# One half of the stream kept on chip between two layers, with two smaller moves, in a two-layer encoder kernel

## The chip, the core and the metric

The kernel runs on one core of a Trainium2 chip. The core has five engines that work side by side, each in its own order: TensorE (PE, matrix products; its weight loads are listed as PEld), VectorE (DVE), ScalarE (ACT), GpSimd (POOL) and SyncE (SP, which here only issues DMA transfers). Transfers are also issued by POOL, and only POOL issues those that add into DRAM while they write. The metric is the device time of one execution in microseconds (us), median over runs. TensorE's clock is granted by a throttle, and the profile shows it as a share of full speed.

## The reference

A float32 stream x of 1024 tokens by 1024 features goes through two layers. Each layer has a mixer and an MLP, both behind an RMSNorm and both added to the stream. Layer 0's mixer is a gated linear recurrence, layer 1's a forgetting attention; in both a 4-head attention into 256 memory tokens stands beside it, and both groups read one projection of the normed stream.

```python
for layer in range(DEPTH):
    h = rms_norm(x, norm_mix[layer])
    y_mix, xq = rglru_group(h, ...) if layer == 0 else fox_group(h, ...)
    y_mem = memory_group(xq, mem, ...)       # keys, values: rms_norm(mem) @ w_kv
    x = x + jnp.concatenate([y_mix, y_mem], axis=-1) @ w_out[layer]
    h = rms_norm(x, norm_mlp[layer])
    x = x + jnp.square(jax.nn.relu(h @ w_mlp_in[layer])) @ w_mlp_out[layer]
```

## The kernel before, in words

**Layout.** The stream is held transposed: 8 row tiles of 128 features, each with two halves of 512 tokens (`H = 512`). Between the stages it lies in DRAM, in `xs` (the tile is named `xspill` in the profile), and is loaded by `load_x`, one row tile and one half at a time (128x512 float32, 256 KB). On chip such tiles live in 86 slots (`NU`), which the float32 tiles `f` and the split tiles `r` share; `get` takes a slot that has been free long, `put` gives it back, and the next user of a slot waits for its last reader.

**Products.** Float32 accuracy is made from three products of split operands: each operand is a high part (`split`, L488: an ACT copy that rounds and applies the norm's gain) and a low part (the rest, made on DVE or POOL, L491 and L499). For weights the same is done in a ring of three buffers, `wh` by ACT (L319) and `wl` by DVE or POOL (L320), from four raw buffers `wr`, which SP fills from DRAM (L315, about one load per weight row). TensorE's result goes to PSUM banks in four groups: `pspj` (2 banks), `pss` (2), `pspt` (3), `pso` (1).

**Norms.** RMSNorm's gain is applied when x is split, its factor 1/rms per token after the product. Sums of squares come in three ways. `sqacc` squares a tile on ACT (L441) and adds it to a running sum on DVE or POOL (L447). `sq_pe` squares on ACT (L452) and lets TensorE add, by products of 128x128 with a column of 1/D (`sq_mm`, L465, 4 narrow products a tile, into a `pso` bank); it keeps the newest two squares back and multiplies those before. `tok_sums` (L469) loads the stream with tokens on the partitions (`xtok`, an input) and lets ACT sum the squares along the row. `norm_fin` turns the sums into the factor and spreads it over the partitions by a scaled identity, made on POOL (L530), and a product with ones (L381).

**Order of the stages.** Layer 0: first half normed and projected (`in_u0`, `in_g0`), recurrence, memory attention, second half, output projection, MLP. Beside `in_g0` the generator `norm_split(1, ...)` (L541) loads and splits the second half of x, and at its end `tok_sums` sums that half's squares; `norm_fin(1, True)` (L1659) follows after the first half's recurrence. The MLP runs in 8 groups of 512 hidden features. Each group multiplies by two 2x2 block matrices in 7 products in place of 8 (operands b11, b21, t2, t3, t1, t4, b22, which are sums and differences of blocks made on DVE): `mlp_z` for the first matrix, `mlp_out` for the second. In `mlp_out` each quarter of the result gets two products: `first` copies the one from PSUM to an `f` slot (L1075, on ACT), `then` adds the other (`plus`, L1080, on DVE), and `send` (L1219) adds the sum into `xs` in DRAM by an accumulating transfer that POOL issues (L1220). So the stream after the last group of layer 0 stands in DRAM alone.

**The seam between the layers.** The generator `kv(1)` makes the memory's keys and values for layer 1 (K: 8 weight rows of 512 columns and products with the normed memory, then norm and transposes; V likewise). It starts inside the last MLP group and is taken 6 steps further at L1682; the rest is woven with `norm_split_back` (L553), which loads the first half of x from `xs` row by row (L538), splits it behind the newest weight split (L488), and sums its squares. Then comes the first projection of layer 1, the memory query (`xq_proj`).

**Who sets the order.** The program is written in stages and generators (`weave`, `advance`, `drain`), but a scheduler then orders each engine's instructions by a modelled time; `after` adds a fixed order between two instructions. So an edit in one place can move instructions far from it.

## Time and profile before

| | us |
|---|---|
| median of 3 runs (lowest, highest) | 2108.54 (2106.35, 2111.91) |
| the profiled execution, and its span | 2108.65, 2106.9 |
| PE busy | 2055.2 (98% of the span), 10378 products |
| DVE busy | 1564.0 (74%) |
| ACT busy | 1154.3 (55%) |
| POOL busy | 463.3 (22%) |
| mean granted clock of TensorE | 0.988 |

Engine totals count busy time over the whole span. Times in the traces run from the span's start. A row of the timeline has start, length, engine, line, operation, tiles, count and, in brackets, how long the engine waited before it and for whom. A row of the waits has who waited for whom, the sum, the count and the longest. A window row is explained where the first one stands.

### The profile page before, as it was taken

The numbers are of one execution on the slowest core, as the hardware profiler recorded it, in microseconds if no ns is written. First come the engines' busy times: TensorE is split into PE (matmuls) and PEld (weight loads), VectorE is DVE, ScalarE is ACT, GpSimd is POOL, SyncE is SP. The second block draws the span as 40 slices with busy tenths as digits, with TensorE's granted clock in tenths as the row PEclk, the third lists the DMA queues.
The fourth block names the chain that finished last, engine by engine and source line by source line (L and its number), as shares of the span: only waits on it lengthen the run. The fifth ranks groups of instructions, "written<-read, shape, count | busy, mean of one in ns | idle before, by whom it ended". The sixth has DMA issues, their size and how long they took to land. (4 is left out here: it accounts for less than half of the span.)

```text
span 2106.9 us, 29666 instructions
## 1 busy us (share of the span) xinstructions
PE 2055.2 (98%) x10378; PEld 1712.8 (81%) x10378; DVE 1564.0 (74%) x2916; ACT 1154.3 (55%) x2172; POOL 463.3 (22%) x590
## 2 busy tenths in 40 slices
PE   9999999999999999997999999999999999999999
PEld 7987788888788888876998998777778888888887
DVE  8878698776776776785585778787787768658757
ACT  7756656554554554555464655576554555445544
POOL 1132210201201201214252333232012122022021
PEclk9999999999999999998899999999999999999999
DMA  7433362635635635748568437743446674365374
GB/s 276 151 99 117 101 195 76 130 81 110 131 81 110 135 77 109 160 94 246 192 232 295 151 100 267 239 149 117 145 101 140 139 179 95 80 147 99 78 184 120
DMA packets 122646, 301.56 MB, mean 143 GB/s; under 512 B 13760, under 2 KB 15872, under 8 KB 122496
## 3 DMA queue, kind: packets, MB, share of 16 engines
q1 hardware_dynamic: 79584, 209.41, 29.6%
q0 software_dynamic: 42912, 90.26, 22.8%
q8 instruction: 81, 1.33, 0.3%
q14 instruction: 69, 0.57, 0.1%
HBM read 190.46 MB, written 109.15 MB: 142 GB/s over the span
## 5 line engine op out<-in xcount | busy, mean ns | idle before, releaser
L1064 PE MATMUL pspt<-r,wh 128*128 128x512 f32 x1536 | 491.6, 396 | 1.0 <-ACT wh L319 1.0
L320 DVE TENSOR_TENSOR wl<-wr,wh 128x1024 fp32r<-128x1024 f32 (+2 forms) x354 | 337.9, 965 | 198.0 <-ACT wh L319 196.9
L319 ACT ACTIVATE wh<-wr 128x1024 fp32r<-128x1024 f32 (+3 forms) x403 | 304.5, 777 | 296.4 <-PE pss L1064 73.2
L1220 POOL DMA_DIRECT2D xspill<-f x240 | 212.1, 1111 | 854.8 <-DVE f L1080 825.1
L1064 PEld LDWEIGHTS pspt<-r,wh 128*128 128x128 f32 x1536 | 288.3, 188 | 71.5 <-ACT wh L319 1.4
L1064 PE MATMUL pss<-r,wh 128*128 128x512 f32 x1024 | 329.1, 396 | 0.4 <-DVE r L499 0.4
L1064 PE MATMUL pspt<-r,wl 128*128 128x512 f32 x768 | 304.0, 396 | 0.0
L1064 PE MATMUL pspj<-r,wh 128*128 128x512 f32 x832 | 272.1, 399 | 1.0 <-DVE r L491 1.0
L388 PE MATMUL pspj<-wh,r 128*128 128x256 f32 (+1 forms) x1280 | 252.5, 290 | 15.3 <-ACT r L488 11.7
L499 DVE TENSOR_TENSOR r<-f,r 128x512 fp32r<-128x512 f32 x282 | 191.0, 696 | 75.9 <-DMA xspill<-f 61.3
L1064 PEld LDWEIGHTS pss<-r,wh 128*128 128x128 f32 x1024 | 192.1, 188 | 48.5 <-DVE r L499 0.8
L388 PEld LDWEIGHTS pspj<-wh,r 128*128 128x128 f32 x1280 | 207.1, 194 | 19.7 <-ACT r L488 13.0
L496 ACT ACTIVATE r<-f 128x512 fp32r<-128x512 f32 x282 | 169.6, 625 | 82.8 <-DMA xspill<-f 25.1
L1064 PE MATMUL pss<-r,wl 128*128 128x512 f32 x512 | 202.4, 395 | 0.0
L1064 PEld LDWEIGHTS pspj<-r,wh 128*128 128x128 f32 x832 | 156.6, 189 | 39.8 <-DVE r L491 1.8
L388 PE MATMUL pspj<-wl,r 128*128 128x256 f32 (+1 forms) x640 | 184.9, 289 | 0.2 <-POOL wl L320 0.2
L1064 PEld LDWEIGHTS pspt<-r,wl 128*128 128x128 f32 x768 | 144.5, 188 | 35.2
L1064 PE MATMUL pspj<-r,wl 128*128 128x512 f32 x416 | 164.9, 397 | 0.0
L388 PE MATMUL pspj<-r,wh 128*128 128x512 f32 x480 | 157.8, 404 | 3.9 <-DVE wr L836 1.7
L1085 ACT ACTIVATE f<-f 128x512 f32<-128x512 f32 x128 | 78.8, 626 | 105.1 <-DVE f L1084 102.8
L388 PEld LDWEIGHTS pspj<-wl,r 128*128 128x128 f32 x640 | 123.7, 193 | 1.2 <-POOL wl L320 0.4
L1064 PEld LDWEIGHTS pss<-r,wl 128*128 128x128 f32 x512 | 96.2, 188 | 23.8 <-issue 0.5
(301 smaller groups left out, 3570.2 us busy)
## 6 DMA issues: line engine op xcount, KB each, us to landing
wr<-in_w_dram SPq DMA_DIRECT2D x136, 512.0 KB, 3.9
xspill<-f POOLq DMA_DIRECT2D x240, 256.0 KB, 7.2
f<-xspill SPq DMA_DIRECT2D x88, 256.0 KB, 4.6
xspill<-f SPq DMA_DIRECT2D x48, 256.0 KB, 3.1
wsp<-wh SPq DMA_DIRECT2D x22, 512.0 KB, 5.7
wsp<-wl SPq DMA_DIRECT2D x22, 512.0 KB, 6.1
wh<-wsp POOLq DMA_DIRECT2D x21, 512.0 KB, 5.2
wl<-wsp POOLq DMA_DIRECT2D x21, 512.0 KB, 5.4
```

The lines of the kernel that those rows point to most:

```text
L319: self.wact = self.nc.scalar.activation(hi, raw, AF.Copy)
L320: eng.tensor_tensor(lo, raw, hi.bitcast(F32), ALU.subtract)
L388: self.lastmm = self.nc.tensor.matmul(out, lhsT=a, rhs=b, start=(j == 0), stop=(j == n - 1))
L496: i = self.nc.scalar.activation(hi[:, :n], src, AF.Copy)
L499: self.nc.vector.tensor_tensor(lo[:, :n], src, hi[:, :n].bitcast(F32), ALU.subtract)
L1064: self.lastmm = self.nc.tensor.matmul(ps, lhsT=a, rhs=b, start=(start and c == 0 and j == 0), stop=(c == n - 1 and j == 2), skip_group_che ...
L1085: self.lastsq = self.nc.scalar.activation(f[:, n], f[:, n], AF.Square)
L1220: nc.gpsimd.dma_start(self.xs[2 * q + a, :, b * H:(b + 1) * H], f[:, n], accum_op=ALU.add)
```

## The change

It has three parts.

1. *First half's result stays on chip.* In the last MLP group of layer 0, when the first matrix is at its operand t1 (`hook7`), the eight row tiles of the first half are loaded from `xs` into `xres`. The two quarters of the result with b = 0, which are these tiles, are then not copied and sent: `held` adds both products into the resident tile on DVE, and the sum is written to `xs` by a plain transfer that SP issues. `norm_split_back` takes the resident tiles and loads nothing. `kv` is taken 2 steps ahead instead of 6.
2. *Second half's row sums.* `tok_sums` issues all its loads first, each into a slot of its own, and then squares. For the second half it is called at the start of `in_g0`, behind the newest weight split on ACT, in place of the end of `norm_split`. `norm_fin(1, True)` moves from behind the first half's recurrence into `in_g0`.
3. *Sums of squares.* `sq_pe` no longer multiplies; it only squares and queues. The narrow products are placed by hand: in layer 0 at operands b11 and b21 of the MLP's first matrix, in layer 1 before and behind the waiting product (`drain(p)` in `mlp`: one MLP group's first matrix, begun ahead of the MLP, that still waits for the last operands of the second half), and the rest in `norm_fin_g`. The `pso` bank is taken when the first of them is made.

```diff
--- before.py
+++ after.py
@@ -218,6 +218,7 @@
         self.parked = {}
         self.stp = {}
         self.tst = {}
+        self.xres = {}
         self.xg = [None, None]
         self.ymix = [None, None]
         self.hs = [None, None]
@@ -453,11 +454,12 @@
         if behind is not None:
             self.after(i, behind)
         if m == 0:
-            self.stp[h] = self.psum("o"), []
+            self.stp[h] = [None, []]
         self.stp[h][1].append((m, sq))
-        self.sq_mm(h, 2)
 
     def sq_mm(self, h, keep):
+        if self.stp[h][0] is None:
+            self.stp[h][0] = self.psum("o")
         st, todo = self.stp[h]
         while len(todo) > keep:
             m, sq = todo.pop(0)
@@ -469,15 +471,17 @@
     def tok_sums(self, src, n, tag, behind=None):
         nc = self.nc
         st = self.small(2 * n, tag, 1)
+        xs = [self.F.get() for _ in range(2 * n)]
+        for k, x in enumerate(xs):
+            nc.sync.dma_start(x[:, :H], src[k // 2, :, k % 2 * H:(k % 2 + 1) * H])
         for t in range(n):
             for j in range(2):
-                x = self.F.get()
-                nc.sync.dma_start(x[:, :H], src[t, :, j * H:(j + 1) * H])
+                x = xs[2 * t + j]
                 i = nc.scalar.activation(x[:, :H], x[:, :H], AF.Square, scale=1.0 / math.sqrt(D),
                                          accum_out=st[:, j * n + t:j * n + t + 1])
                 if behind is not None:
                     self.after(i, behind)
-                self.F.put(x)
+        self.F.put(*xs)
         return st
 
     def tok_var(self, v, st, n):
@@ -538,7 +542,7 @@
         self.nc.sync.dma_start(x[:, :H], src[k, :, h * H:(h + 1) * H])
         return x
 
-    def norm_split(self, h, g, src, stats, tok=None):
+    def norm_split(self, h, g, src, stats):
         xs = self.xg[h] = []
         for k in range(8):
             x = self.load_x(k, h, src)
@@ -547,14 +551,12 @@
             xs.append(self.split(x[:, :H], self.pc(g, k)))
             self.F.put(x)
             yield
-        if tok is not None:
-            self.tst[h] = self.tok_sums(tok[4 * h:4 * h + 4], 4, f"tst{h}", self.last_hi)
-
-    def norm_split_back(self, h, g, src):
+
+    def norm_split_back(self, h, g):
         nc = self.nc
         xs = self.xg[h] = [None] * 8
         for j, k in enumerate((0, 2, 4, 6, 1, 3, 5, 7)):
-            x = self.load_x(k, h, src)
+            x = self.xres.pop(k)
             xs[k] = self.split(x[:, :H], self.pc(g, k), behind=self.wact)
             self.sqacc(j, h, x[:, :H], nc.vector, self.last_hi)
             self.F.put(x)
@@ -1226,7 +1228,20 @@
             nc.sync.dma_start(self.out[2 * q + a, :, b * H:(b + 1) * H], f[:, n])
             self.F.put(f)
 
+        def held(a):
+            def first(q, ps):
+                self.plus(self.xres[2 * q + a], ps)
+
+            def then(q, ps):
+                x = self.xres[2 * q + a]
+                self.plus(x, ps)
+                nc.sync.dma_start(self.xs[2 * q + a, :, :H], x[:, n])
+
+            return first, then
+
         def keep(a, b):
+            if b == 0 and self.xres:
+                return held(a)
             dst = []
 
             def first(q, ps):
@@ -1274,19 +1289,25 @@
         def hook0(key):
             if key in ahead:
                 self.xsplit(ahead[key])
+            if key in ("b11", "b21"):
+                self.sq_mm(1, 6 if key == "b11" else 3)
             if key in ("t2", "t3"):
                 advance(nf)
 
         def hook7(key):
             if key == "t2" and nxt is not None:
                 advance(nxt)
+            if key == "t1" and not l:
+                self.xres = {m: self.load_x(m, 0, self.xs) for m in (0, 2, 4, 6, 1, 3, 5, 7)}
             if key == "t1" and l:
                 self.acc = [self.load_x(2 * q, 0, self.xs) for q in range(4)]
 
         for p in wait:
             for k in ("t3", "t1"):
                 self.xsplit(k)
+            self.sq_mm(1, 5)
             drain(p)
+            self.sq_mm(1, 2)
         for g in range(8):
             if g == 0 and g in self.parked:
                 for k in ("t3", "t1"):
@@ -1591,7 +1612,7 @@
 
 
         xk = self.ins["xtok"]
-        nrm = [self.norm_split_first(0, "gmix0", xT, xk), self.norm_split(1, "gmix0", xT, False, xk)]
+        nrm = [self.norm_split_first(0, "gmix0", xT, xk), self.norm_split(1, "gmix0", xT, False)]
         advance(nrm[0])
         kv = self.kv(0)
 
@@ -1623,7 +1644,10 @@
                     yield
 
         def in_g0():
+            self.tst[1] = self.tok_sums(xk[4:], 4, "tst1", self.wact)
             for m in range(4):
+                if m == 2:
+                    self.norm_fin(1, True)
                 for _ in range(4):
                     advance(kv)
                     yield
@@ -1656,7 +1680,6 @@
         weave(self.xq_proj(0), lru0, TUNE["xq0"])
         drain(lru0)
         self.xg_free(0)
-        self.norm_fin(1, True)
         xa0 = self.xattn(0)
         weave(self.xq_proj(1), xa0, TUNE["xq1"])
         weave(in_u1(), xa0, TUNE["in_u1"])
@@ -1679,8 +1702,8 @@
 
 
         self.fox_setup()
-        advance(kv, 6)
-        weave(kv, self.norm_split_back(0, "gmix1", self.xs), 1.0)
+        advance(kv, 2)
+        weave(kv, self.norm_split_back(0, "gmix1"), 1.0)
         self.vst = {}
         xq = self.xq_proj(0, 1)
         advance(xq, 4)
```

The lines behind the edits move by one to four: L1080 is L1082 in the changed kernel, L499 is L503, L488 is L492, L530 is L534.

**Where it moves instructions: DVE in the last group of layer 0's MLP.** The rows are DVE's order, from the place where the second matrix's first products are out. Names are tile, generation, number; L1188 to L1196 before (L1187 to L1198 in the changed kernel) make the operand sums, L499 (L503) their low parts, L320 (L321) and L629 (L631) low parts of weights and of the memory, L1082 is the plus. Before:

```order
L1188 TENSOR_TENSOR f40_835_7958<-f21_824_7841,f7_816_7732 128x512
L1194 TENSOR_TENSOR f41_834_7954<-f21_824_7841,f41_834_7954 128x512
L320 TENSOR_TENSOR wl2_78<-wr0_69,wh2_75 128x1024
L1188 TENSOR_TENSOR f8_839_7980<-f53_825_7855,f83_817_7746 128x512
L1194 TENSOR_TENSOR f37_838_7976<-f53_825_7855,f37_838_7976 128x512
L629 SCALAR_TENSOR_TENSOR r9_853_8086<-f81_818_7782,par_79,r51_852_8085 128x256 x2
L1196 TENSOR_TENSOR f60_822_7808<-f60_822_7808,f40_835_7958 128x512
L499 TENSOR_TENSOR r17_855_8092<-f7_816_7732,r56_854_8091 128x512
L499 TENSOR_TENSOR r11_857_8096<-f83_817_7746,r52_856_8095 128x512
L499 TENSOR_TENSOR r75_837_7961<-f40_835_7958,r76_836_7960 128x512
```

In the changed kernel four pluses into resident tiles stand among the operand sums:

```order
L1082 TENSOR_TENSOR f41_830_7865<-f41_830_7865,pss_397_8006 128x512
L1187 TENSOR_TENSOR f12_816_7732<-f8_842_7970,f12_816_7732 128x512
L1082 TENSOR_TENSOR f22_832_7869<-f22_832_7869,pspj_399_8008 128x512
L503 TENSOR_TENSOR r53_841_7953<-f15_823_7822,r30_840_7952 128x512
L1082 TENSOR_TENSOR f39_831_7867<-f39_831_7867,pss_398_8007 128x512
L1187 TENSOR_TENSOR f31_817_7746<-f5_846_7992,f31_817_7746 128x512
L1082 TENSOR_TENSOR f48_833_7871<-f48_833_7871,pspj_400_8009 128x512
L1190 TENSOR_TENSOR f71_843_7974<-f20_824_7841,f12_816_7732 128x512
```

and directly behind them:

```order
L1196 TENSOR_TENSOR f8_842_7970<-f20_824_7841,f8_842_7970 128x512
L321 TENSOR_TENSOR wl2_78<-wr0_69,wh2_75 128x1024
L631 SCALAR_TENSOR_TENSOR r11_857_8098<-f67_818_7782,par_79,r52_856_8097 128x256 x2
L503 TENSOR_TENSOR r72_859_8104<-f12_816_7732,r73_858_8103 128x512
L1190 TENSOR_TENSOR f54_847_7996<-f84_825_7855,f31_817_7746 128x512
L1196 TENSOR_TENSOR f5_846_7992<-f84_825_7855,f5_846_7992 128x512
L503 TENSOR_TENSOR r62_861_8108<-f31_817_7746,r61_860_8107 128x512
L1082 TENSOR_TENSOR f41_830_7865<-f41_830_7865,pspt_401_8051 128x512
L1198 TENSOR_TENSOR f37_822_7808<-f37_822_7808,f71_843_7974 128x512
L1082 TENSOR_TENSOR f39_831_7867<-f39_831_7867,pspt_402_8052 128x512
L1082 TENSOR_TENSOR f22_832_7869<-f22_832_7869,pspt_403_8053 128x512
L503 TENSOR_TENSOR r19_845_7977<-f71_843_7974,r78_844_7976 128x512
```

The split that ends the last list (`r19`) is the one that ends the first (`r75` there). It now stands 19 rows behind the first plus, and seven of these rows are pluses; before, no plus stood ahead of it.

**ACT at the seam.** The rows are ACT's order around the split of the first rows of x for layer 1 (L488, its square L441). Before, they follow the key transposes' copies (L677), one row of x after another:

```order
L677 ACTIVATE r72_929_8748<-pspt_425_8745,gkq_409_8343 128x256
L677 ACTIVATE r39_930_8754<-pspt_426_8751,gkq_409_8343 128x256
L488 ACTIVATE r32_912_8598<-f63_911_8596,par_79 128x512
L441 ACTIVATE f36_914_8602<-f63_911_8596 128x512
L488 ACTIVATE r63_916_8620<-f36_915_8618,par_79 128x512
L441 ACTIVATE f0_918_8624<-f36_915_8618 128x512
L488 ACTIVATE r36_920_8643<-f0_919_8641,par_79 128x512
L441 ACTIVATE f37_922_8647<-f0_919_8641 128x512
```

In the changed kernel the splits (L492, L442) read the resident tiles `f41`, `f39`, `f22` and stand among the memory's copies and the weight splits (L320) of the key/value stage:

```order
L492 ACTIVATE r0_888_8395<-f41_830_7865,par_79 128x512
L442 ACTIVATE f33_890_8399<-f41_830_7865 128x512
L1077 ACTIVATE f44_883_8332<-pspj_400_8009 128x512
L492 ACTIVATE r41_891_8414<-f39_831_7867,par_79 128x512
L442 ACTIVATE f65_893_8418<-f39_831_7867 128x512
L601 ACTIVATE f26_885_8354<-pspt_411_8366 128x256
L320 ACTIVATE wh0_73<-wr3_72 128x256 x2
L603 ACTIVATE f27_887_8392<-f26_885_8354 128x256
L320 ACTIVATE wh0_73<-wr3_72 128x256
L492 ACTIVATE r65_895_8437<-f22_832_7869,par_79 128x512
L442 ACTIVATE f49_897_8441<-f22_832_7869 128x512
L320 ACTIVATE wh0_73<-wr3_72 128x256
```

All eight pairs moved in front of the key transposes.

**POOL in layer 0's first projection.** The rows are POOL's order around the scaled identity of the second half's norm (L530, L534 in the changed kernel); L890 and L901 belong to the recurrence, L706 to the memory attention's query. Before:

```order
L890 TENSOR_SCALAR f77_136_1207<-f77_136_1207 128x512
L706 TENSOR_TENSOR f68_129_1174<-f68_129_1174,xr_109_1516 128x512
L706 TENSOR_TENSOR f69_130_1175<-f69_130_1175,xr_109_1516 128x512
L706 TENSOR_TENSOR f33_131_1176<-f33_131_1176,xr_109_1516 128x512
L706 TENSOR_TENSOR f72_132_1177<-f72_132_1177,xr_109_1516 128x512
L890 TENSOR_SCALAR f63_133_1201<-f63_133_1201 128x512
L530 TENSOR_SCALAR f38_157_1546<-ident_81,rst1_112_1534 128x128 x4
L901 TENSOR_SCALAR f63_133_1201<-f63_133_1201 128x512
```

In the changed kernel:

```order
L534 TENSOR_SCALAR f35_105_888<-ident_81,rst1_83_876 128x128 x4
L892 TENSOR_SCALAR f34_135_1225<-f34_135_1225 128x512
L892 TENSOR_SCALAR f85_136_1227<-f85_136_1227 128x512
L892 TENSOR_SCALAR f0_137_1229<-f0_137_1229 128x512
L892 TENSOR_SCALAR f71_134_1223<-f71_134_1223 128x512
L903 TENSOR_SCALAR f71_134_1223<-f71_134_1223 128x512
```

The four scaled identities now stand ahead of the recurrence's rows.

## The prediction

> **What bounds the kernel now.** I read the page's engine totals first, then the stages in 40 us windows, then PE's waits, and last the two engines around the places that stood out.
>
> ```profile
> PE 2055.2 (98%) x10378; PEld 1712.8 (81%) x10378; DVE 1564.0 (74%) x2916; ACT 1154.3 (55%) x2172; POOL 463.3 (22%) x590
> PEclk9999999999999999998899999999999999999999
> ```
>
> TensorE is busy for 2055.2 of 2106.9 us, so only 51.7 us are plain waiting, and the clock row dips in just one place, a little before the middle. The windows (columns: stretch, its length, busy time and count for PE, PEld, DVE, ACT, POOL, then granted clock, DMA share, GB/s) put both in one stage:
>
> ```profile
> 960.00:1000.00 40.00, 27.07 (x193) 24.44 (x193) 24.97 (x52) 22.58 (x60) 14.78 (x16) 0.83 0.80 259
> 1000.00:1040.00 40.00, 36.25 (x256) 35.63 (x255) 19.60 (x53) 14.61 (x40) 9.82 (x10) 0.79 0.47 169
> ```
>
> This is the seam between the layers: memory keys and values of layer 1, then the first query projection. PE idles 12.9 us in the first window, and the clock is low in both. The list of PE's waits names the cause, and the waits of 920 to 1060 us say what stands behind it (us, times, longest):
>
> ```profile
> PE pspj L388 <- ACT r L488: 11.7, 4, 5.4
> PE pso L381 <- POOL f L530: 3.1, 1, 3.1
> PE pso L465 <- ACT f L452: 2.8, 1, 2.8
> ACT r L488 <- DMA f<-xspill: 23.1, 7, 7.1
> SPq L538 <- DVE f L447: 21.9, 5, 7.9
> ```
>
> PE waits for the split of x (L488), the split for its load from DRAM, and the load for a buffer: only one slot is free, and it comes back when DVE has added the previous square (L447). So one row of x after another makes a round trip, while the clock falls to half:
>
> ```profile
> 990.00:995.00 5.00, 2.93 (x12) 2.63 (x12) 1.35 (x2) 1.24 (x2) 0.00 (x0) 0.50 0.99 345
> 1010.00:1015.00 5.00, 5.00 (x25) 4.96 (x24) 2.95 (x15) 1.27 (x4) 0.00 (x0) 0.50 0.01 3
> ```
>
> At 1010 PE is busy throughout and yet does 25 products in 5 us, where at full clock (1017 to 1040, below) it does 197 in 23, or 43 in 5: the low clock goes on costing after the waits are over.
>
> **The change, part by part.** *The seam (removes).* The eight loads are issued during the last MLP group, the x rows wait in SBUF, and the order puts all eight splits among the weight splits of the key/value stage instead of after it. The price of the old stage, from its first product at 956.6 to the return of the clock at 1017, and beside it the same kind of product at full speed:
>
> ```profile
> 956.60:1017.00 60.40, 43.72 (x280) 40.43 (x279) 31.02 (x71) 27.56 (x70) 17.23 (x19) 0.75 0.62 196
> 1017.00:1040.00 23.00, 23.00 (x197) 23.00 (x197) 13.55 (x33) 10.86 (x32) 9.82 (x10) 1.00 0.75 270
> L388 PE MATMUL pspt<-wh,r 128*128 128x256 f32 x128 | 23.2, 281 | 0.6 <-ACT f L599 0.6
> L388 PE MATMUL pspt<-wl,r 128*128 128x256 f32 x64 | 18.1, 286 | 0.3 <-DVE wl L320 0.3
> L388 PE MATMUL pspj<-wh,r 128*128 128x256 f32 x47 | 16.1, 421 | 11.7 <-ACT r L488 11.7
> L388 PE MATMUL pspj<-wl,r 128*128 128x256 f32 x24 | 9.6, 398 | 0.0
> L675 PE MATMUL pspt<-ident,f 128*128 128x128 f32 x8 | 2.4, 380 | 4.1 <-DVE r L668 2.6 <-DVE f L659 1.4
> L381 PE MATMUL pso<-cD,f 128*128 128x1 f32 x8 | 1.8, 347 | 0.0
> L488 ACT ACTIVATE r<-f,par 128x512 fp32r<-128x512 f32 x8 | 5.8, 721 | 23.1 <-DMA f<-xspill 23.1
> L441 ACT ACTIVATE f<-f 128x512 f32<-128x512 f32 x8 | 4.9, 615 | 0.0
> ```
>
> 128+64+47+24 = 263 products; at 23.00/197 = 0.117 us each they need 30.7 us. The eight transposes and eight narrow products took 2.4 and 1.8 us at partly half clock; I take 2.9 us for both. So 33.6 us of work stood in 60.4 us, and at most 26.8 us are to be had. How much is given back depends on ACT and DVE, which must now do their 27.6 and 31.0 us in those 33.6 us: both fit, ACT at 82%, DVE at 92%. But ACT is in order, and each split and square (0.72 and 0.62 us, the last two rows) may stand ahead of a weight split that PE is about to need. In the old stage such delays cost 0.6 and 0.3 us (the first two L388 rows). Bounds: 1 us and 10 us (eight pairs of 1.3 us, each fully exposed). I take 3, nearer the low end, since PE's order now also has query products to run while the key transposes wait. **−23.8 us.**
>
> *The pluses (moves).* In the last group, the first adds of two quarters were ACT copies; they are now DVE additions. DVE is full just there, and PE was already waiting for it:
>
> ```profile
> 920.00:925.00 5.00, 5.00 (x23) 4.00 (x23) 5.00 (x9) 4.67 (x9) 0.00 (x0) 1.00 0.03 7
> 920.19 0.68 DVE L320 TENSOR_TENSOR wl<-f,wh 128x512 fp32r<-128x512 f32 x1
> 920.79 0.69 DVE L1185 TENSOR_TENSOR f<-f,f 128x512 f32<-128x512 f32 x1
> 923.80 1.22 DVE L320 TENSOR_TENSOR wl<-wr,wh 128x1024 fp32r<-128x1024 f32 x1
> 926.13 0.88 DVE L629 SCALAR_TENSOR_TENSOR r<-f,par,r 128x256 fp32r<-128x256 f32 x2
> 929.48 0.50 PE L1064 MATMUL pss<-r,wh 128*128 128x512 f32 x1 [0.39 <-DVE r L499]
> ```
>
> Rows of this shape follow each other every 0.60 us (920.19 to 920.79), 0.09 less than they last; the eight pluses are thus 4.8 us. The product at 929.48 needs the low half of the operand whose split ends the DVE piece shown ahead. In the old order the row at 920.79 has the place that the first plus has in the new one. From there 19 rows stand ahead of that split: 17 × 0.60, one full weight row (1.22 − 0.09) and one pair (0.88 − 0.09) make 12.1 us, so it starts at 932.9 and ends at 933.6. PE takes three other products first, some 0.23 us each, and gets there at about 929.6, so it waits 4.0 us where it waited 0.4. Bounds: 0 (the lateness is absorbed) and 8 (the 4.0 us, and as much lost at a low clock). The ACT time set free and the smaller DMA load (eight plain writes for eight accumulating ones) shorten nothing that PE waited for. **+4.0 us.**
>
> The trace leaves open whether a 4 us wait also lowers the clock: a wait of 3.07 us up to 134 us left it at 1.00, one of 2.77 us up to 1511 us was followed by half clock (rows of both below). I add half of 1.8 us, what some 3.5 us at half clock lose. **+0.9 us.** [...]
>
> *Second half's row sums and norm.* Eight loads of xtok are issued together, and the scale of the second half is made before the recurrence instead of behind it. On POOL it now stands ahead of L890 and L901 where it stood behind five rows of other work, so the wait goes:
>
> ```profile
> 134.20 1.12 PE L381 MATMUL pso<-f,ones 128*128 128x512 f32 x2 [3.07 <-POOL f L530]
> 120.00:160.00 40.00, 35.77 (x208) 30.74 (x207) 36.16 (x72) 21.96 (x40) 15.44 (x12) 1.00 0.28 86
> 0.00:350.00 350.00, 337.18 (x1830) 284.56 (x1831) 288.04 (x627) 225.59 (x464) 63.08 (x80) 1.00 0.46 149
> ```
>
> **−3.1 us.** The eight squares stay on ACT and its idle time covers them; without cover they are 8 × 0.6 = 4.8 us. The scheduler reorders PE in nearly the whole stretch up to 330 us. PE's other idle time before 350 is 350 − 337.2 − 3.1 = 9.7 us and could shrink or grow; I take 0, from −4 to +6.
>
> *Sums of squares among the products.* Their count stays, but PE no longer stops for the newest square:
>
> ```profile
> 1509.90 0.69 DVE L945 TENSOR_TENSOR f<-f,pspt 128x512 f32<-128x512 f32 x1 [1.55 <-DMA f<-xspill]
> 1511.31 1.45 PE L465 MATMUL pso<-cD,f 128*128 128x1 f32 x8 [2.77 <-ACT f L452]
> 1512.00:1516.00 4.00, 4.00 (x12) 3.25 (x13) 3.29 (x6) 2.19 (x5) 0.00 (x0) 0.50 0.38 144
> 1516.00:1520.00 4.00, 4.00 (x16) 3.19 (x15) 3.21 (x5) 3.10 (x6) 0.00 (x0) 0.67 0.35 131
> 1520.26 1.29 DVE L499 TENSOR_TENSOR r<-f,r 128x512 fp32r<-128x512 f32 x2
> ```
>
> The wait and the low clock after it cost 2.8 + 2.0 + 1.3 = 6.1 us. But what is late next is the last quarter of the MLP's operands, ready at 1521.5 after a load that came late; PE would reach it about 6 us earlier and wait there. Bounds −6.1 and 0; I take half. **−3.0 us.** In layer 0, where no wait was, 0.
>
> Sum: −23.8 + 4.0 + 0.9 − 3.1 − 3.0 = −25.0. The profiled execution took 2108.65 us (span 2106.9 and 1.75 around it), the median of the runs is 2108.54: **2083.6, say 2084 us.**
>
> **Rivals.** *The key/value stage becomes bound by ACT and the weights* (chance 0.20). For it: 27.6 us of ACT in order, POOL doing half of the low parts, and a DMA share of 0.99 in the 990 row. Against: ACT sat idle 23.1 us there for loads alone. Price: the residue is 10 to 15 instead of 3, so 2091 to 2096.
>
> *The early stretch gets worse* (0.10). For it: DVE is busy 288 of those 350 us, and SP's new order brings the eight token loads ahead of two weight loads. Against: the work is the same. Price +6 on the 0 taken and the 3.1 kept by another wait: 2093.
>
> *The loads block SP* (slower, 0.03). Four of the new loads take slots that the previous group's accumulating transfers still read; until those land, the second-layer weights queue behind them on SP. The first of these, issued at 885.6 and landing 3.9 us later, now has 10 us to its split:
>
> ```profile
> 878.19 4.37 POOL L1220 DMA_DIRECT2D xspill<-f  x5 [4.68 <-ACT f L1075]
> 885.57 17.06 SPq L315 DMA_DIRECT2D wr<-in_w_dram  x4
> 899.96 1.06 ACT L319 ACTIVATE wh<-wr 128x1024 fp32r<-128x1024 f32 x1 [1.97 <-PE pss L1064]
> wr<-in_w_dram SPq DMA_DIRECT2D x136, 512.0 KB, 3.9
> xspill<-f POOLq DMA_DIRECT2D x240, 256.0 KB, 7.2
> ```
>
> Against: the last of those transfers is issued within the 4.4 us after 878.2 (first row), and with a landing of 7.2 us it holds SP some 4 us. Beyond 10 us of blocking PE begins to lose, at 35 the gain of 25 is gone, and at 45 the time is 2119.
>
> *The change doesn't do what it says* (0.04): the seam waits for weights instead, PE idles as long, and only the 6 us of the two small edits remain: 2103, within measurement.
>
> **How the numbers follow.** The forecast has 0.63. Its terms may miss by −2 to +7 (seam), ±4 (pluses), ±1 (clock), −4 to +6 (early) and ±3 (squares); as independent errors, root of squares, −7 to +10: 2077 to 2094. The range that should hold 8 in 10 goes a little wider for the first two rivals: 2074 to 2097. About 0.3% (6 us) is what a measurement of this kernel can tell from none. Faster by more: 0.63 + 0.20 + 0.10 = 0.93; same 0.04; slower 0.03.
>
> **What would show it.** Right: the clock row without its dip, no wait of PE for a split of x at the seam, PE busy nearly 40 of 40 us in the windows after 960, and a wait of about 4 us for a DVE split near 930; no wait of 3 us for POOL before 140; at most half of the 2.8 us for a square in layer 1, with a wait for an MLP operand behind it. Wrong: PE waits in the key/value stage of over 10 us in sum, or more idle time before 350 us than the 12.8 there now.

## The result, and the profile after

The changed kernel takes 2083.02 us (median of 4 runs, 2080.89 to 2085.55) where the kernel before takes 2108.97 in the same runs. The ratio is 0.9877, with a 95% interval of 0.9859 to 0.9895, or 26 us less. The forecast was 2084. That the sum came out to 1 us is in part luck: the seam and the early stretch gained 6.3 us more than forecast, the other terms 4.5 less, and two of the reasons given were wrong.

The page of the changed kernel, engine totals and clock row:

```profile
PE 2046.6 (98%) x10378; PEld 1706.1 (82%) x10378; DVE 1569.0 (75%) x2924; ACT 1148.5 (55%) x2164; POOL 456.6 (22%) x582
PEclk9999999999999999999999999999999999999999
```

The dip in the middle is gone. PE is busy for 8.6 us less with as many products, since fewer of them run at half clock (mean granted clock 0.996 against 0.988), and idle for 18.0 us less (33.7 instead of 51.7). The windows (columns as in the prediction):

```profile
0.00:350.00 350.00, 341.82 (x1854) 289.12 (x1855) 291.91 (x633) 228.05 (x469) 66.43 (x84) 1.00 0.46 152
960.00:1000.00 40.00, 40.00 (x339) 39.63 (x338) 34.28 (x79) 28.60 (x78) 17.65 (x20) 1.00 0.85 279
1000.00:1040.00 40.00, 40.00 (x340) 39.95 (x340) 28.75 (x76) 24.94 (x73) 19.62 (x26) 1.00 0.70 252
```

In the seam PE now works without a gap at full clock, 679 products in 80 us where there were 449. Before 350 us PE idles 8.2 us instead of 12.8. Two rows of PE's waits answer to those quoted before:

```profile
PE pspt L1066 <- DVE f L1082: 2.9, 2, 2.3
PE pso L382 <- POOL f L534: 0.3, 1, 0.3
```

The wait for POOL is down from 3.1 to 0.3 us. New is a wait for a plus (L1082).

To place the gain I compare the starts of the same products in both traces: one in the second MLP group of layer 0, the first key/value product, and the first small transpose (L1401, L1422 now) of layer 1's attention. Before:

```profile
406.97 0.63 PE L1064 MATMUL pspt<-r,wh 128*128 128x512 f32 x2
956.64 0.28 PE L388 MATMUL pspt<-wh,r 128*128 128x256 f32 x1
1103.42 0.27 PE L1401 MATMUL pspt<-ident,cc 128*32 128x128 f32 x1
```

After:

```profile
400.92 0.63 PE L1066 MATMUL pspt<-r,wh 128*128 128x512 f32 x2
955.97 0.28 PE L389 MATMUL pspt<-wh,r 128*128 128x256 f32 x1
1075.64 0.27 PE L1422 MATMUL pspt<-ident,cc 128*32 128x128 f32 x1
```

So 6.1 us are gained up to the second MLP group, 5.4 lost up to the first key/value product, 27.1 gained in the seam. The last MLP product ends at 2075.7 instead of 2102.5, 26.8 us earlier: what follows the seam in layer 1, where squares were moved, took 1.0 longer. The same three products and that end measure the experiments (us, difference from the kernel before in its profiled execution):

| kernel | up to the 2nd MLP group | rest of layer 0's MLP | seam | after it | ratio to before (95%) |
|---|---|---|---|---|---|
| the change | −6.1 | +5.4 | −27.1 | +1.0 | 0.9877 (0.9859–0.9895) |
| first part alone | +1.4 | +5.3 | −26.8 | +4.1 | 0.9916 (0.9901–0.9931) |
| second part alone | −4.4 | +0.2 | +1.0 | +3.9 | 0.9983 (0.9972–0.9993) |
| third part alone | −1.3 | +0.3 | −2.0 | +2.4 | 0.9989 (0.9979–0.9998) |
| POOL adds | −5.4 | +0.8 | −25.9 | +1.4 | 0.9852 (0.9837–0.9867) |
| loads together only | +0.7 | −0.2 | −22.9 | +4.4 | 0.9906 (0.9891–0.9921) |
| 2 steps only | +0.5 | −0.3 | −6.5 | +1.5 | 0.9976 (0.9964–0.9987) |
| the change with 6 steps | −6.0 | +5.2 | −22.0 | +1.4 | 0.9905 (0.9889–0.9922) |
| the change, not resident | −6.7 | +0.2 | −23.9 | +1.5 | 0.9859 (0.9844–0.9873) |

The four columns of stages compare single executions, all with the same one of the kernel before, and one step of 3.41 us at half clock more or less shifts an entry by 1.7 us. The ratios rest on all runs.

### The profile page after: what moved, and what is told of

Its sections match the earlier page's. It is cut to its first block, busy times and chain, and to the rows that moved or that the text cites. A ratio compares the mean times of both kernels' runs of the same rounds, so it can differ in the third digit from the quotient of the medians.

```text
span 2080.3 us, 29644 instructions
## 1 busy us (share of the span) xinstructions
PE 2046.6 (98%) x10378; PEld 1706.1 (82%) x10378; DVE 1569.0 (75%) x2924; ACT 1148.5 (55%) x2164; POOL 456.6 (22%) x582
## 5 line engine op out<-in xcount | busy, mean ns | idle before, releaser
L321 DVE TENSOR_TENSOR wl<-wr,wh 128x1024 fp32r<-128x1024 f32 (+2 forms) x354 | 338.3, 964 | 182.7 <-ACT wh L320 181.5
L320 ACT ACTIVATE wh<-wr 128x1024 fp32r<-128x1024 f32 (+3 forms) x403 | 303.5, 776 | 301.6 <-PE pss L1066 77.0
L1222 POOL DMA_DIRECT2D xspill<-f x232 | 203.1, 1071 | 871.6 <-DVE f L1082 802.5
L389 PE MATMUL pspj<-wh,r 128*128 128x256 f32 (+1 forms) x1280 | 244.3, 285 | 2.1 <-DVE fl L1390 0.8
L503 DVE TENSOR_TENSOR r<-f,r 128x512 fp32r<-128x512 f32 x282 | 188.6, 685 | 71.8 <-DMA xspill<-f 52.0
L389 PEld LDWEIGHTS pspj<-wh,r 128*128 128x128 f32 x1280 | 201.8, 189 | 4.7 <-PE pspj L389 1.0
```

What stands on the lines that cost most here:

```text
L320: self.wact = self.nc.scalar.activation(hi, raw, AF.Copy)
L321: eng.tensor_tensor(lo, raw, hi.bitcast(F32), ALU.subtract)
L389: self.lastmm = self.nc.tensor.matmul(out, lhsT=a, rhs=b, start=(j == 0), stop=(j == n - 1))
L503: self.nc.vector.tensor_tensor(lo[:, :n], src, hi[:, :n].bitcast(F32), ALU.subtract)
L1222: nc.gpsimd.dma_start(self.xs[2 * q + a, :, b * H:(b + 1) * H], f[:, n], accum_op=ALU.add)
```

## The experiments

**The three parts, each alone.** Each edit is one of the three parts of the diff, applied to the kernel before.

> The first part of the change alone (resident rows, eight pluses, key/value stage 2 steps ahead); norm sums and squares as before. Theory (the parts act in their own stages): the first 350 us are those of before with their wait of 3.1 us for POOL, the wait of some 3 us and the low clock near 930 appear (+5), the seam loses 27; 2109 + 5 - 27 = 2087 us, between 2083 and 2091. Rival (the seam's gain needs the other two parts, since the scheduler reorders everything): PE waits of over 8 us in the seam, 2095 us or more.

It took 2092.29 us, ratio 0.9916, 5 us more than the first theory said and outside its range. The table shows the two terms it named, +5.3 and −26.8, so they belong to this part alone; the rival falls. What the theory missed are 1.4 us in the early part and 4.1 after the seam. The late ones arise at the squares of layer 1, where PE now waits 5.7 us for the newest square; before, it waited 2.8 (PE's wait, 1475 to 1515 us):

```profile
PE pso L466 <- ACT f L453: 5.7, 1, 5.7
```

The early one is instructive. The wait for POOL is as long as before, 3.07 us, but here half clock follows it. PE's row in the first part alone, and the window of 3.41 us that holds most of the wait, with the next:

```profile
136.83 2.02 PE L382 MATMUL pso<-f,ones 128*128 128x512 f32 x2 [3.07 <-POOL f L531]
133.51:136.92 3.41, 0.34 (x4) 0.14 (x2) 3.02 (x7) 1.04 (x3) 3.41 (x4) 1.00 0.00 0
136.92:140.33 3.41, 3.41 (x10) 2.38 (x11) 2.94 (x6) 1.37 (x3) 1.02 (x2) 0.50 0.00 0
```

In the kernel before the same wait lies across the border of two such windows, counted back in steps of 3.413 us from that execution's first low step, at 313.7 us; the clock is 1.00 in both and in the next:

```profile
129.41:132.82 3.41, 1.72 (x15) 1.51 (x13) 3.41 (x8) 1.83 (x4) 3.41 (x4) 1.00 0.28 113
132.82:136.23 3.41, 2.03 (x12) 1.56 (x13) 2.55 (x3) 1.50 (x3) 2.50 (x3) 1.00 0.00 0
```

In the three other kernels with the old order (third part alone, loads together, 2 steps only) a low step begins at this place too, at 135.5, 136.3 and 135.9 us. The execution of the kernel before is the exception. The steps are measured with the blocks of narrow products below.

> The second part alone (row sums loaded together, second half's norm earlier). Theory of the prediction: the POOL wait of 3.1 us goes and nothing else, 2106 us. Second theory, from the trace after the change (6 us gained before the second MLP group): the reordering gains some 3 us more by shorter waits of other kinds, 2103 us. Rival: the scheduler's new order gives it back elsewhere in the first 350 us, 2109 us. The start of the second MLP group, 407 us before, tells them apart: 404, 401 or 407.

2108.74 us, ratio 0.9983. The product that stands at 407.0 before comes at 402.5, between the two theories (404 and 401): the POOL wait is gone, and 1.3 us more. Layer 1 gives most of it back in the profiled execution (+3.9 in the last column): at the squares PE waits 5.3 us in sum where it waited 2.8, and the mean clock of this execution is 0.986 where it was 0.988; the ratio over 8 runs says 3.6 us less.

> The third part alone (sums of squares placed by hand). Theory of the prediction: 3 us less in layer 1, where the wait for the newest square goes, nothing in layer 0; 2106 us. Second theory, from the trace after the change: layer 1 gains nothing, because the last quarter of the MLP's operands is late and takes the wait over; what is gained is the low clock near 315 us (1.7 us) if the narrow products there no longer stand in one block; 2107 us. Rival: no effect at all, 2109 us.

2108.41 us, ratio 0.9989, 2.3 us less. In layer 1 the wait for the newest square is gone, and PE waits for an MLP operand in its place:

```profile
PE pspt L1065 <- ACT r L497: 1.5, 1, 1.5
PE pspt L1065 <- DVE r L500: 0.8, 2, 0.6
```

That is the second theory's wait. The 2 us in the seam column cannot come from the squares, which stand elsewhere; in that column the low clock (0.50) lasted 6 steps of 3.4 us, from 985.4 to 1005.9 us, and 1 more, from 1009.3 to 1012.7, against 9 before, from 986.2 to 1016.9.

**Four pluses taken off DVE.** The changed kernel, with the first quarter's two products summed in a scratch tile and added to the resident tile by POOL:

```diff
 def first(q, ps):
-    self.plus(self.xres[2 * q + a], ps)
+    if a == 0: self.copies(tmp)(q, ps)          # ACT
+    else: self.plus(self.xres[2 * q + a], ps)
 def then(q, ps):
-    self.plus(x, ps)
+    if a == 0:
+        self.plus(tmp[q], ps)
+        nc.gpsimd.tensor_tensor(x[:, n], x[:, n], tmp[q][:, n], ALU.add)
+    else: self.plus(x, ps)
```

> The changed kernel, but the first quarter's two products go through a scratch tile as they did before (ACT copy, then plus), and POOL adds the sum to the resident tile: four pluses fewer on DVE, four adds more on POOL. Theory (PE waits near 925 for DVE to empty the PSUM banks, since the four new pluses stand ahead): the wait of 2.9 us and the low clock behind it go, 5 us less than the changed kernel, 2078 us. Rival A (what is late is the operand split, and other work on DVE takes the place of the pluses): at most 1 us less, 2082. Rival B (POOL's adds delay the weights' low parts or slow DVE in the key/value stage): 2083 or more, with waits for low parts after 955 us.

2079.81 us, ratio 0.9852. The last group's +5.4 shrinks to +0.8, so the pluses were the stall. Waits of PE from 915 to 1045 us, and POOL's row there:

```profile
PE pss L1066 <- DVE f L1082: 0.7, 1, 0.7
PE pspj L389 <- DVE r L495: 0.5, 1, 0.5
924.53 8.03 POOL L1244 TENSOR_TENSOR f<-f,f 128x512 f32<-128x512 f32 x4 [18.66 <-DVE f L1082]
```

POOL's four adds take 8.0 us, but POOL had stood idle for 18.7. Rival B's price is there and small: the seam loses 1.2 us against the change.

The same kernel again, beside the changed kernel on one chip:

> The kernel with the first quarter's scratch tile and POOL adds once more, beside the changed kernel on the same chip. Theory (the stall near 925 and its low clock were worth 4 to 5 us): ratio to the kernel before 0.985 to 0.987, and 3 to 5 us less than the changed kernel in the same call. Rival (the first result was luck of the clock's steps): as long as the changed kernel within 1.5 us.

> The changed kernel itself, as the measure for the run before it in this call: ratio to the kernel before 0.987 to 0.989, 2081 to 2086 us.

2081.05 and 2084.34 us, ratios 0.9856 (0.9841 to 0.9871) and 0.9875 (0.9860 to 0.9890). The difference is 3.3 us here; by the ratios it was 5 us in the first comparison (0.9852 and 0.9877) and is 4 now. The intervals overlap a little, the stages in the traces agree (last group +0.9 against +4.8 here).

**What the seam's gain hangs on.** First the kernel before with the eight loads issued together, nothing resident, and 2 steps instead of 6:

```diff
-for j, k in enumerate((0, 2, 4, 6, 1, 3, 5, 7)):
-    x = self.load_x(k, h, src)
+ord8 = (0, 2, 4, 6, 1, 3, 5, 7)
+xr = {k: self.load_x(k, h, src) for k in ord8}
+for j, k in enumerate(ord8):
+    x = xr[k]
...
-advance(kv, 6)
+advance(kv, 2)
```

> The kernel before, with one edit at the seam: nothing is kept on chip, the last group still adds into DRAM, but the eight rows of x are asked for together, each into a slot of its own, and the key/value generator is taken 2 steps ahead instead of 6. Theory A (the old seam paid for one slot's round trips): the loads come close behind each other, all eight splits stand among the key/value work, the seam loses some 20 us without the pluses' cost: 2089 us. Theory B (the rows must first have landed in DRAM, so only rows kept on chip can be early): the first load does not come back before some 970 us, PE still waits over 10 us for splits and the clock still drops, 2100 us or more.

2089.47 us, ratio 0.9906: theory A. That it fits to half a microsecond is luck, since the seam gained 22.9 us instead of 20 and the stretch after it lost 4.4. The loads on SP's queue and the window of the seam:

```profile
934.64 2.48 SPq L538 DMA_DIRECT2D f<-xspill  x2
940.67 1.97 SPq L538 DMA_DIRECT2D f<-xspill  x2
959.00 1.44 SPq L538 DMA_DIRECT2D f<-xspill  x2
961.49 1.81 SPq L538 DMA_DIRECT2D f<-xspill  x2
960.00:1000.00 40.00, 37.03 (x300) 35.39 (x299) 35.32 (x76) 28.26 (x77) 19.64 (x24) 1.00 0.88 284
```

All eight rows are asked for by 963.3 us, four of them while the last group still runs. They could be had from DRAM early enough all along.

Then each of the two edits by itself: the 2 steps in the kernel before (`advance(kv, 6)` becomes `advance(kv, 2)`, nothing else),

> The kernel before with one number changed: the key/value generator is taken 2 steps ahead of the first split of x instead of 6; the loads still go one row at a time through one slot. Theory (the round trips of the single slot were the cost): PE still waits some 10 us for splits and the clock drops, 2105 to 2110 us. Rival (the loads were late only because the splits stood behind the whole key/value work): most of the gain of the loads issued together is there already, 2095 us or less.

which took 2105.15 us, ratio 0.9976. Waits of 915 to 1045 us and the window:

```profile
PE pspj L388 <- ACT r L488: 7.3, 3, 4.5
960.00:1000.00 40.00, 29.09 (x209) 26.49 (x208) 27.00 (x54) 22.70 (x60) 15.06 (x17) 0.87 0.83 267
```

PE still waits 7.3 us for splits and idles 10.9 us in this window. The theory holds, with 6.5 us of the seam for the 2 steps. The loads together with the 6 steps were not run. For the other direction, the changed kernel with 6 steps:

> The changed kernel with the key/value generator taken 6 steps ahead of the first split as before, in place of 2: the first splits of x stand some rows later in the program. Theory (the rows wait on chip, so the exact place of their splits costs little): within 2 us of the changed kernel, 2083 to 2085, PE busy all through 960 to 1040. Rival (the place of the splits was half of the gain): PE waits for splits of x (L492) at the end of the key/value stage, 5 us or more, 2088 or more.

2089.00 us, ratio 0.9905, 6 us slower than the change. My theory here falls: with the rows on chip, the place of their splits still decides over 5 us. The rival's place was not right either. PE does not wait for L492; it loses 2.4 us to several small waits and one step at half clock:

```profile
960.00:1000.00 40.00, 37.63 (x298) 36.35 (x297) 35.30 (x77) 29.61 (x78) 18.38 (x20) 0.96 0.69 238
986.00:990.00 4.00, 4.00 (x21) 3.84 (x22) 3.94 (x8) 2.53 (x5) 0.00 (x0) 0.57 1.02 416
```

Last, the changed kernel without its residency: the last group copies and sends as before, the eight loads go together at the seam.

```diff
-            if key == "t1" and not l:
-                self.xres = {m: self.load_x(m, 0, self.xs) for m in (0, 2, 4, 6, 1, 3, 5, 7)}
...
-            x = self.xres.pop(k)
+            x = xr[k]          # all eight loaded at the generator's start
```

> The changed kernel without its residency: the last group copies and sends the first half's result to DRAM as before, and the eight rows are loaded together at the seam; the other two parts stay. Theory (what counts at the seam is that the eight loads go together; keeping the rows on chip gains some 4 us there and loses 5 to the pluses): equal to the changed kernel within 2 us, 2081 to 2085, with no wait near 925 and waits of some 3 us in sum between 955 and 1020. Rival (residency carries the gain once the rest of the kernel has changed): 2090 us or more.

2081.05 us, ratio 0.9859 (0.9844 to 0.9873), 3.3 us less than the change beside it. Its seam:

```profile
960.00:1000.00 40.00, 37.74 (x312) 36.73 (x312) 30.75 (x74) 25.30 (x71) 14.45 (x17) 1.00 0.82 296
```

Some 2.3 us of small waits remain here that the change does not have, and the last group keeps its old time (+0.2 against +5.4). Keeping the rows on chip therefore gained 3.2 us in the seam and cost 5.2 ahead of it. The theory's range held, but not its "equal within 2 us": the kernel without residency is the faster one.

**Blocks of narrow products.** Into the changed kernel, in layer 0's MLP where PE never waits, went twelve gapless blocks of extra 128x128 by one-column products, the shape of the sums of squares, with unused results:

```diff
+            if l == 0 and key in ("b21", "t3") and 0 < g < 7:
+                self.block((8, 16, 24, 32, 48, 24, 32, 24, 32, 24, 48, 32)[2 * g - (2 if key == "b21" else 1)])
             yield from self.product(banks, xp[key], start, done)
```

> The changed kernel with twelve blocks of extra narrow products (128x128 with one column, each block without a gap, result unused) among the wide products of layer 0's MLP, where PE never waits: 8, 16, 24, 32, 48, 24, 32, 24, 32, 24, 48 and 32 of them, 344 in all, at 0.11 us each 39 us. Theory (the clock is decided on a fixed grid of 3.41 us, and a stretch of the grid that is mostly filled by narrow products counts as idle): blocks of 8 and 16 (0.9 and 1.8 us) are followed by no low clock, those of 48 (5.5 us) always, by one or two steps of 3.41 us, and those of 24 and 32 (2.7 and 3.6 us) only where most of the block lies in one step of the grid; low stretches start and end at multiples of 3.41 us from each other. Each low step costs 1.7 us: some 2083 + 39 + 8 x 1.7 = 2136 us. Rival (narrow products count as work): no low clock behind any block, 2122 us. Second rival (the low clock follows a block's length, not the grid): all blocks of 24 alike, and all of 32 alike.

2212.25 us (one run), far more than any theory's sum. I had taken a narrow product for 0.11 us; that is one record, and each product leaves two (a block of 8 shows 16), so 0.23 us, and the blocks were twice as long as I wrote. 344 × 0.23 = 79 us of them, and an estimated 60 us lost by a mean clock of 0.969 over 2210.5 us where the changed kernel has 0.996 over 2080.3 (2210.5 × 0.031 − 2080.3 × 0.004), make 139; 129 were measured. With the lengths corrected, the grid theory holds for the five low stretches that I placed: they start at 422.27, 497.36, 627.07, 726.07 and 821.64 us, the later ones 22, 60, 89 and 117 times 3.413 us behind the first. Steps of the grid, busy time of these narrow products alone (PE, PEld), clock, DMA share, GB/s:

```profile
405.20:408.62 3.42, 1.84 (x16) 1.94 (x16) 1.00 1.08 195
408.62:412.03 3.41, 0.00 (x0) 0.00 (x0) 1.00 0.63 174
719.24:722.66 3.42, 1.95 (x19) 2.13 (x19) 1.00 0.50 153
722.66:726.07 3.41, 3.41 (x32) 3.39 (x31) 1.00 0.48 153
726.07:729.48 3.41, 0.06 (x1) 0.00 (x0) 0.50 0.00 1
818.23:821.64 3.41, 2.09 (x20) 2.28 (x20) 1.00 0.21 84
821.64:825.05 3.41, 3.41 (x18) 3.41 (x17) 0.50 0.49 154
```

Two blocks of 24. The one of 720 us puts 1.95 us into one step and fills the next: full clock after the first, half after the second. The one of 819 us puts 2.09 us into its first step, and the clock is halved at once. So in this run a step with 2.09 of its 3.41 us in narrow products is followed by a step at half clock, and one with 1.95 is not. No sharp limit is shown: in the kernel with the loads together, the sums of squares fill 2.10 us of one step, and the next keeps full clock (these products alone):

```profile
1470.91:1474.32 3.41, 2.10 (x20) 2.29 (x20) 1.00 0.71 218
1474.32:1477.74 3.42, 1.53 (x14) 1.44 (x13) 1.00 0.39 138
```

Both rivals fall: half clock follows the step that narrow products fill (3.41 of 3.41 us, from 722.66), and the two blocks of 24 differ.

**Weight sums on POOL in layer 1.** The kernel with POOL adds and `u.dve = l == 0 or g > 0` in place of `u.dve = True` for the first matrix.

> The kernel with the first quarter's scratch tile and POOL adds, and one edit more: the sums and differences of weight blocks for the first group of layer 1's MLP are made on POOL, which stands idle from 1448 to 1496 us, instead of on DVE. Theory (in layer 1 the squares' new place gains nothing because DVE is full and makes the last operands of the MLP late): DVE loses some 4 us of work ahead of those operands, PE's waits of 3 us near 1480 and the low clock behind them (3.4 us) go in part, 2 to 5 us less than without the edit, 2075 to 2078. Rival (POOL is slower, the weights' halves become late): as much or more waiting near 1475, for weights, 2080 or more.

2082.75 us, ratio 0.9874: 2 to 3 us worse than without the edit (2079.81 and 2081.05), or 4 to 5 by the ratios. Waits from 1440 to 1500 us, and one of POOL's rows:

```profile
PE pspt L1066 <- DVE r L503: 1.8, 3, 1.1
PE pspt L1066 <- DVE wl L321: 1.1, 2, 0.6
PE pspt L1066 <- ACT wh L320: 1.1, 1, 1.1
1474.04 2.80 POOL L360 TENSOR_TENSOR f<-wr,wr 128x512 f32<-128x512 f32 x1 [3.16 <-DVE wl L321]
```

The rival: an addition of 128x512 that takes DVE 0.67 us took POOL up to 2.8, and PE waits for weights. It does not test the theory about DVE cleanly, since it puts another wait in the place of the old one.

## Why the prediction was right, and where it was not

- **The seam: right in kind, under-estimated, and its reason too wide.** −23.8 forecast, −27.1 measured. The term mis-sized is the 3 us "given back" by splits that stand ahead of weight splits: PE gives back nothing (80.00 of 80 us busy, clock 1.00), and the bound of 26.8 us is reached. The chain of one slot and one load at a time was read correctly. But the working took for granted that the rows must be kept on chip for this. Loads issued together from DRAM gain 22.9 us with the 2 steps; the 2 steps alone 6.5. Residency is worth 3 us there.
- **The pluses: right size, wrong place.** +4.0 forecast with +0.9 for the clock, +5.4 measured (+4.8 in the second profile). The forecast made PE wait near 930 for the low half of an operand, 19 rows behind the first plus. In fact PE stops earlier, for a PSUM bank that DVE has not emptied. DVE's order and PE's wait:

```profile
915.10 0.67 DVE L1082 TENSOR_TENSOR f<-f,pss 128x512 f32<-128x512 f32 x1
924.84 0.67 DVE L1082 TENSOR_TENSOR f<-f,pspt 128x512 f32<-128x512 f32 x1
925.65 0.47 PE L1066 MATMUL pspt<-r,wh 128*128 128x512 f32 x1 [2.26 <-DVE f L1082]
```

  The first plus goes at 915.1; the add that empties the bank (it was on DVE before, too) comes at 924.8, behind all that the backlog holds. The wrong step is "The product at 929.48 needs the low half of the operand": of the things that queue behind the pluses I followed one and not the earliest. That the pluses are the cause is shown by the POOL run, which takes four of them away and leaves +0.8, and by the run without residency, which has none of them and +0.2.
- **The clock.** The forecast's half of 1.8 us was a coin toss over a question that the runs settle for this place: the low step came in both executions of the changed kernel, from 928.5 and from 928.0 us. No run shows the 3.5 us at half clock from which the 1.8 was taken; the low step lasted 3.41 us at a clock of 0.50 and cost 1.7. In steps of the grid:

```profile
921.64:925.05 3.41, 1.75 (x8) 1.08 (x6) 3.41 (x8) 2.79 (x5) 0.00 (x0) 1.00 0.52 154
925.05:928.47 3.42, 1.97 (x5) 1.02 (x6) 3.42 (x7) 0.74 (x2) 0.00 (x0) 1.00 0.47 177
928.47:931.88 3.41, 3.41 (x9) 2.64 (x9) 3.41 (x7) 0.21 (x1) 0.00 (x0) 0.50 0.56 158
```

  The step with eight wide products, of which six begin in it (PE busy for 1.75 us), is followed by full clock, the step with five (1.97 us) by half clock. In the second execution a step with ten (2.24 us) is followed by full clock and the next, with four (1.49 us), by half clock. The step ahead of the low one was thus not an idle one in either. The low stretches of the kernel before start at 313.7, 986.2, 1231.9, 1498.2 and 1511.8 us, 351 steps of 3.413 us from the first to the last. The prediction set the wait of 3.07 us, which left the clock at 1.00, beside the one of 2.77 us, which half clock followed. The longer lay across two steps, with PE busy for 1.72 and 2.03 us of them; the shorter lay in one, with PE busy for 0.64 of its 3.41 us, and the two steps behind that one are at 0.50.
- **Row sums and norm: right in kind, under-estimated.** −3.1 forecast, −6.1 measured, of which the second part alone brings 4.4 and the third 1.3. The wait for POOL went as said. The term set to zero, "its other waits", shrank by 1.9 us (12.8 − 8.2 of idle time, less 2.8 of the POOL wait), and the low step that stood at 313.7 us is not there (clock 1.00 from 300 to 350 us), 1.7 us. How much of that step is the order and how much the chance of where the steps lie stays open. Two kernels without the third part have a low step there (before, at 313.7 us; second part alone, at 310.3), and four executions with it have none (the change in both, the POOL adds in the second, the change not resident: clock 1.00 from 300 to 347 us), so the narrow products' new places are the likelier reason.
- **Squares: the wait was taken over, and the gain stays open.** −3.0 forecast as half of the bound. Against the one execution of the kernel before, nothing was gained in layer 1 (+1.0 after the seam). The forecast named what would take over, the last quarter of the operands, and gave it half of the wait; by this comparison it took all. But that execution is a favourable one: the four other kernels of the table without the third part take 1.5 to 4.4 us longer than it after the seam. Those with the third part take 0.8 to 2.4 us longer in seven executions (five kernels, two of them twice). On average that is 2.8 us in the five executions without it (the one of before counted as 0) and 1.3 in the seven with it. So some gain in layer 1 is likely, but none is shown; the runs of the third part alone, 2.3 us less in all, don't say in which layer. In the changed kernel the last results for the last quarter are in PSUM early, and DVE comes late:

```profile
1465.66 2.88 PE L389 MATMUL pss<-r,r 128*128 128x512 f32 x12
1479.71 0.67 DVE L947 TENSOR_TENSOR f<-f,pss 128x512 f32<-128x512 f32 x1
1484.63 0.63 PE L1066 MATMUL pspt<-r,wh 128*128 128x512 f32 x1 [1.54 <-ACT r L500]
```

  The product ends at 1468.5, DVE adds it 11 us later without having been idle ahead of it, and PE waits at 1484.6 for what is made of it. And the narrow products now stand in blocks, one of which costs a step itself:

```profile
1467.70:1471.11 3.41, 2.72 (x24) 2.83 (x24) 1.00 0.09 34
1471.11:1474.52 3.41, 0.01 (x1) 0.00 (x0) 0.51 0.20 77
```

  (these two rows count the narrow products alone). That DVE's backlog is the limit is read from the trace; the run that was to show it moved the limit to the weights.
- **The rivals.** None came about: no wait of PE is listed between 928 and 1045 us, the early stretch got better, SP was not blocked (the eight loads were issued from 868.6 to 887.4 us, and no weight came late for it).

The sum: −6.1 + 5.4 − 27.1 + 1.0 = −26.8 in the spans up to the last MLP product, forecast −25.0. The seam and the early part brought 6.3 us more than forecast, the squares, the pluses and the rest 4.5 less. That these cancel is luck; that the seam carries nearly all of the gain is not.

## What to carry to other kernels

When a stage waits for loads that pass through one buffer, issue them together before anything is restructured to avoid them: that was 16 of the seam's 27 us, the order of the neighbouring work 6, the residency 3 to 4 (counted in this order of edits). The work moved here onto DVE, which feeds TensorE, came back as waiting (+5.4 us), at the first PSUM bank behind it that was needed; of several things queued on such an engine, follow the earliest. The two versions that leave first adds off DVE (POOL adds, or loads together and nothing resident) both take 2081.05 us beside the change's 2084.34. And a term of a few microseconds is not to be read off one execution of each kernel: the one of the kernel before was a favourable one in two places, at the POOL wait and at the squares of layer 1.

## What the runs showed of the hardware

In one execution the low stretches of the granted clock began at multiples of 3.413 us from each other (five in the kernel before, 351 steps from the first to the last; the five placed in the run with the blocks, up to 117 steps apart). Where these steps lay differed from run to run (the changed kernel's first low step began at 928.5 us in one execution and at 928.0 in another; those of the third part alone and of the second run of the POOL adds, at 135.5 and 7.9 us, are 37.4 steps apart). So one and the same wait of 3.07 us cost no low step in the kernel before and one in the first part alone; in three other kernels a low step began at its place. In the run with the blocks, the step behind one filled by products of one column (3.41 us of them) was at half clock; behind 1.95 us of them the clock stayed at 1.00, behind 2.09 it was at 0.50. In the kernel with the loads together it stayed at 1.00 behind 2.10.
